# Releasing the first FFN weights earlier, and holding x and conditioning loads back until they have landed, in an eight-core streaming-encoder kernel

## Chip, cores, metric

One Trainium2 chip, all 8 cores, one launch. Each core computes its own 2048 tokens (a quarter of one of two sequences), with 512 tokens of left context as "block 0"; blocks 1 to 4 are its own tokens. The metric is device time of the slowest core, in microseconds (us). Executions in which one die ran visibly slower at a lower granted clock ("slow state"; in one of 1922.9 us the four cores of one die had a mean clock of 0.815 to 0.817 and those of the other 0.971 to 0.980) are left out of every ratio below; where a median includes one, the text says so.

## The reference, cut to what matters

```python
cc = silu(c)
mod = (cc @ w_ada + b_ada)             # 9 x 1024 conditioning values per sequence
sh1, sc1, gt1, ... = mod
h = rms_norm(x, g_ffn1) * (1 + sc1) + sh1
x = x + 0.5 * gt1 * (silu(h @ w_in[:, :2816]) * (h @ w_in[:, 2816:])) @ w_out
# ... token mixing (chunk-band attention and pooling), then a second FFN of the same form
```

Everything here happens in the first 165 us of some 1660: the conditioning values of the first FFN, the first norms, and the first hidden group of the first FFN.

## The kernel before

Names used below. `w_ada` is stored as 72 "rows" of 128 x 1024. One **dot** on DVE turns one row into 128 conditioning values; dots are counted from 0, so dot 2 is the third. Rows 0 to 15 of the early order give shift and scale of the first FFN and must be done before any hidden unit is complete; rows 16 to 23 give its gate, which is first needed when the first group's outputs are added. `w1i` are the input weights of the first FFN: chunk 0 and chunk 1 each hold two hidden tiles (`jj` 0 and 1), each with an a part and a b part. A **unit** is one hidden tile for one block: 16 matmuls. The first group's input units (5 blocks x 4 units) use chunks 0 and 1 only. x0 to x4 are the five blocks of x; x2, x3 and x4 are 2 MB loads. `w1o` are the output weights of the first FFN, `w_pg` is a small weight of the later token mixing. In the profile lines, `arena` is the one SBUF buffer that holds all tiles, `ps` is PSUM, and the line numbers are those of the helpers that record an operation: L179 matmul, L185 and L186 ScalarE activation, L196 a dot, L215 a load.

```python
    for i in range(16):                                   # early conditioning
        dots.append(ada_dot(aorder[i], ADA_R[i % 6]))     # DVE
        if i + 6 < 16:
            ada_load(aorder[i + 6], ADA_R[i % 6], "d_a%d" % (i % 6))   # SP queue
        # [cut: per pair of dots, scale and shift; statistics and norm of x0, x1]
    for i in range(2):
        ada_load(16 + i, ada_slot(16 + i), "d_b%d" % i)
    for b in range(2, 5):
        P.load("sp", XB[b - 1][:, :, :], xT[b], "d_x%d" % b)
# [cut]
        def wi_load(split=None):                          # POOL queue, casts to bf16
            # [cut]
            if split is not None:
                for jj in range(nt):
                    for s, o in ((sa, 0), (sb, NJ)):
                        P.load("pool", ..., deps=[split[jj]])
                return
            for s, o in ((sa, 0), (sb, NJ)):
                P.load("pool", piece(s)[:, 0:nt, :], ...)
        def pre():
            wi_load(startup)              # chunk 0: waits for dots 2 and 11
        def body():
            wi_load()                     # chunk 1
            wo_load(0)                    # w1o of the first group, needed at about 150 us
            for bi, b in enumerate(blocks):
                for k in range(2):
                    for jj in range(2):
                        unit(k, jj, b, spread if bi == k == jj == 0 else None)
                        side["g0"](bi, 2 * k + jj)        # norms of x2..x4, later dots
# [cut]
    def g0_1(bi, u):
        g0_norms(4 * bi + u, N1)          # x2: squares after unit 1, statistics matmuls after unit 2
        if bi >= 1 and u % 2 == 0:
            ada_step()                    # one later dot, and the load of the row after next
# [cut]
    pre1()
    P.load("pool", WPG[:, :, :], ..., "d_wpg", deps=[dots[15]])
    body1()
```

The kernel's helper gives each engine its instructions in program order. `g0_norms`: behind unit 1 (units count from 0) ACT squares x2, and behind unit 2 PE has the statistics matmuls that read these squares. So PE reaches unit 3 only after x2 is there.

## Time and profile before

| | before |
|---|---|
| median time | 1668.4 us (fast runs 1667.7 to 1671.0) |
| PE busy, share of the chain of waits | 92% of the span, 83% |
| PE waiting for w1i, per core | 14.0 to 16.0 us |
| start of unit 1 / unit 3 / end of the first group's input units | 64.7 / 88.1 / 162.8 us |
| from there to the last matmul | 1491.2 us |

The last two rows are counted matmul by matmul: TensorE runs the same 7085 matmuls in the same order, so the start of the 58th, 94th and 386th can be compared between runs. Two of the eight traces have 140 matmul records missing; such means are over the six full traces.

PE's waits in the first 160 us of the slowest core (core 4):

```profile
PE ps L179 <- ACT arena L186: 25.2, 7, 14.6
PE ps L179 <- ACT arena L185: 23.7, 13, 11.9
PE ps L179 <- DMA arena<-w1i: 16.0, 3, 6.8
```

The three waits for w1i in the timeline of that core's PE (start, length, instructions, and in brackets the idle time before and what ended it):

```profile
59.94 0.59 PE L179 MATMUL ps<-arena 128*128 128x512 bf16 x2 [1.85 <-ACT arena L186]
65.26 3.41 PE L179 MATMUL ps<-arena 128*128 128x512 bf16 x8 [4.73 <-DMA arena<-w1i]
73.16 3.57 PE L179 MATMUL ps<-arena 128*128 128x512 bf16 x8 [4.49 <-DMA arena<-w1i]
83.49 16.82 PE L179 MATMUL ps<-arena 128*128 128x512 bf16 x65 [6.76 <-DMA arena<-w1i]
```

Unit 0 ends at about 60.5 us; unit 1 gets its a half at 65.26, its b half at 73.16, and chunk 1 lands only at 83.49. Eight matmuls take 3.41 or 3.57 us here, twice their usual time (they start every 427 ns; at full clock, later on the same core, every 216 ns). The table by stretches shows why (columns: stretch, its length, busy us and count for PE, PEld, DVE, ACT, POOL, then granted clock, DMA busy share, GB/s):

```profile
50.00:60.00 10.00, 3.92 (x18) 1.34 (x17) 7.35 (x16) 5.46 (x8) 2.33 (x4) 1.00 1.02 292
60.00:70.00 10.00, 3.94 (x10) 1.09 (x10) 0.69 (x1) 5.73 (x8) 2.30 (x4) 0.66 1.03 301
70.00:80.00 10.00, 3.57 (x8) 1.02 (x8) 0.69 (x1) 1.25 (x2) 0.00 (x0) 0.59 1.00 254
80.00:90.00 10.00, 6.51 (x18) 2.39 (x19) 0.09 (x1) 0.60 (x1) 0.00 (x0) 0.56 0.96 161
90.00:100.00 10.00, 10.00 (x48) 4.57 (x47) 1.59 (x3) 7.08 (x8) 0.00 (x0) 1.00 0.01 3
```

The granted clock, the first of the last three numbers, falls to about 0.6 from 60 to 90 us (0.66, 0.59, 0.56) and returns to 1.00. Its records hold only 1.00 and 0.50, and each spell of half clock in the first 165 us lasts 3.4 us or a multiple of it. In this trace gaps of 4.5 to 6.8 us were followed by matmuls of double length, and the gap of 1.9 us was not (two matmuls in 0.59 us).

The DMA engines are full from 50 to 85 us (a busy share of 0.98 to 1.08 in each 5 us), and most of what fills them is x2 to x4: 6.3 of the 9.9 MB written from 47 to 85 us. They are issued at 47.1 to 49.2 us and land after 16, 23 and 28 us; w1i issued at 51.7 lands after 13.5 and 20.8 us, and at 59.5 after 23.9 and 25.9 us.

### The profile page before, as it was taken

Reading aid. Unit: us, or ns where it says so; the run is one execution under the profiler, and the core shown is the slowest. Engines: PE = TensorE matmul, PEld = TensorE weight load, DVE = VectorE, ACT = ScalarE, POOL = GpSimd, SP = SyncE. Lnnn points to the kernel's source line nnn. Section 1 sums busy time; section 2 is a strip of 40 time slices with the busy share of each in tenths; the row PEclk is TensorE's granted clock in tenths of the full one; section 3 lists DMA queues with packets and bytes.
Section 4 is the critical chain, followed back from the end, with each engine's and each line's share of the span. In section 5 each row is a group of like instructions: output and inputs, shape, how many; then the busy total and the mean of one; then the engine's idle time right before and its main releaser. Section 6 shows DMA issues by size and latency. Waiting matters only on the chain.

```text
span 1667.4 us, 20421 instructions; the slowest of 8 cores (1653.6 to 1667.4 us)
## 1 busy us (share of the span) xinstructions
PE 1537.1 (92%) x7085; PEld 672.7 (40%) x7085; DVE 820.2 (49%) x1300; ACT 480.2 (29%) x615; POOL 95.7 (6%) x191
## 2 busy tenths in 40 slices
PE   1498999999999998898799998799999999999999
PEld 0133444444444443342244432244434444444444
DVE  4446736447346346735745445645456161613416
ACT  3354010110110114655644165644150101011110
POOL 0101000010010000000011100001101000001000
PEclk9799999999999998898899998799999999999999
DMA  9923353161370353030054530044504313104005
GB/s 280 267 54 88 62 123 80 39 140 33 90 145 10 89 127 75 1 51 1 1 89 76 88 51 1 1 89 77 88 1 76 51 26 57 26 14 83 13 1 202
DMA packets 45938, 119.50 MB, mean 72 GB/s; under 512 B 4112, under 2 KB 4240, under 8 KB 45328
## 3 DMA queue, kind: packets, MB, share of 16 engines
q0 software_dynamic: 31152, 59.91, 21.8%
q1 hardware_dynamic: 14688, 58.30, 10.7%
q8 instruction: 60, 0.98, 0.2%
q14 instruction: 38, 0.31, 0.1%
HBM read 169.70 MB, written 8.39 MB: 107 GB/s over the span
## 4 chain that ended last, share of the span: by engine, by line
PE 83%; DVE 5%; ACT 4%; DMA 4%; issue 3%; SPq 0%; DVEq 0%; ACTq 0%; POOL 0%
PE ps L179 83%; ACT arena L185 3%; DMA arena<-w_ada 2%; DVE arena L189 2%; DVE arena L194 2%; DMA arena<-w1i 1%; DVE arena L196 1%; ACT arena L186 1%; SPq L215 0%; DVE arena L209 0%; ACT L185 0%; ACT L186 0%; DVE arena L201 0%; DVEq L173 0%; DVE arena L205 0%
## 5 line engine op out<-in xcount | busy, mean ns | idle before, releaser
L179 PE MATMUL ps<-arena 128*128 128x512 bf16 (+5 forms) x7085 | 1537.1, 380 | 126.4 <-ACT arena L185 37.1
L179 PEld LDWEIGHTS ps<-arena 128*128 128x128 bf16 (+1 forms) x7085 | 672.7, 99 | 990.3 <-issue 246.6
L185 ACT ACTIVATE arena<-ps 128x512 bf16<-128x512 f32 (+4 forms) x368 | 271.0, 745 | 911.1 <-PE ps L179 903.7
L189 DVE TENSOR_TENSOR arena<-arena,ps 128x512 bf16<-128x512 bf16 (+1 forms) x230 | 175.2, 762 | 560.8 <-PE ps L179 493.3
L194 DVE SCALAR_TENSOR_TENSOR arena<-ps,arena 128x512 f32<-128x512 f32 (+1 forms) x410 | 315.5, 774 | 155.3 <-PE ps L179 80.2
L185 ACT ACTIVATE arena<-arena 128x1024 bf16<-128x1024 f32 (+2 forms) x105 | 95.2, 929 | 37.5 <-PE ps L179 15.8
L196 DVE SCALAR_TENSOR_TENSOR arena<-arena 128x1024 f32<-128x1024 f32 x72 | 87.8, 1220 | 32.4 <-DMA arena<-w_ada 18.3
L189 DVE TENSOR_TENSOR arena<-arena 128x512 bf16<-128x512 bf16 (+9 forms) x191 | 89.9, 494 | 27.0 <-ACT arena L185 19.6
L186 ACT ACTIVATE arena<-arena 128x512 bf16<-128x512 f32 (+1 forms) x84 | 57.5, 715 | 124.8 <-DVE arena L194 103.1
L194 DVE SCALAR_TENSOR_TENSOR arena<-arena 128x512 f32<-128x512 f32 (+2 forms) x114 | 78.9, 728 | 1.9 <-ACT arena L186 0.5
L215 POOL DMA_DIRECT2D arena<-w1i x26 | 17.1, 660 | 520.0 <-PE ps L179 470.2
L189 DVE TENSOR_TENSOR arena<-ps,arena 64x512 bf16<-64x512 f32 x32 | 22.0, 688 | 43.4 <-ACT arena L185 43.0
L215 POOL DMA_DIRECT2D arena<-w3i x24 | 16.3, 678 | 380.3 <-PE ps L179 380.3
L215 POOL DMA_DIRECT2D arena<-w_in x28 | 19.8, 707 | 297.3 <-PE ps L179 297.3
L186 ACT ACTIVATE arena<-ps,arena 128x1024 f32<-128x1024 f32 (+1 forms) x32 | 29.6, 926 | 17.4 <-PE ps L179 17.2
L185 ACT ACT_TABLE_LOAD x14 | 18.0, 1283 | 43.7 <-PE ps L179 36.5
L201 DVE TENSOR_SCALAR arena<-arena 128x512 bf16<-128x512 f32 (+2 forms) x45 | 19.8, 441 | 6.0 <-DMA arena<-cst 1.0
L212 POOL MEMSET arena<- 64x128 bf16 x64 | 11.9, 198 | 166.8 <-ACT arena L185 166.8
L186 ACT ACT_TABLE_LOAD x12 | 15.4, 1283 | 13.4 <-PE ps L179 13.3
L201 DVE TENSOR_SCALAR arena<-ps,arena 128x512 bf16<-128x512 f32 (+2 forms) x25 | 15.6, 638 | 4.6 <-PE ps L179 4.4
L209 DVE CAST arena<-ps 128x256 bf16<-128x256 f32 x32 | 12.0, 418 | 4.3 <-PE ps L179 4.0
L215 POOL DMA_DIRECT2D arena<-w_o x8 | 5.6, 704 | 73.8 <-PE ps L179 73.8
(14 smaller groups left out, 51.5 us busy)
## 6 DMA issues: line engine op xcount, KB each, us to landing
arena<-w_ada SPq DMA_DIRECT2D x72, 512.0 KB, 4.3
arena<-w_in POOLq DMA_DIRECT2D x28, 512.0 KB, 6.1
arena<-w3i POOLq DMA_DIRECT2D x20, 512.0 KB, 6.3
arena<-w1i POOLq DMA_DIRECT2D x18, 512.0 KB, 10.0
outT<-arena SPq DMA_DIRECT2D x16, 512.0 KB, 3.0
arena<-xT SPq DMA_DIRECT2D x3, 2048.0 KB, 23.0
arena<-w1o POOLq DMA_DIRECT2D x10, 512.0 KB, 16.5
arena<-w3o POOLq DMA_DIRECT2D x10, 512.0 KB, 9.6
```

What stands on the lines that cost most here:

```text
L179: return self.op("pe", lambda e: e.matmul(out, lhsT=lhsT, rhs=rhs, start=start, stop=stop), reads=[lhsT, rhs], writes=[out])
L185: return self.op("act", lambda e: e.activation(out=out, in_=in_, func=func, scale=scale), r, [out])
L186: return self.op("act", lambda e: e.activation(out=out, in_=in_, func=func, bias=bias, scale=scale), r, [out])
L189: return self.op(eng, lambda e: e.tensor_tensor(out=out, in0=in0, in1=in1, op=op), [in0, in1], [out])
L194: return self.op("dve", lambda e: e.scalar_tensor_tensor(out=out, in0=in0, scalar=scalar, in1=in1, op0=op0, op1=op1), r, [out])
L196: return self.op("dve", lambda e: e.scalar_tensor_tensor(out=out, in0=in0, scalar=scalar, in1=in1, op0=op0, op1=op1, accum_out=accum), r, ...
L201: return self.op(eng, lambda e: e.tensor_scalar(out=out, in0=in0, scalar1=s1, scalar2=None, op0=op0), r, [out])
L209: return self.op(eng, lambda e: e.tensor_copy(out=out, in_=in_), [in_], [out])
L212: return self.op(eng, lambda e: e.memset(out, v), [], [out])
L215: return self.op(q, lambda e: e.dma_start(out=out, in_=in_), [], [out], deps, sem)
```

## The change

Its intent: the weights that PE is about to need should not share the DMA engines with x blocks and rows needed later. The weights are released earlier (dots 1, 7, 11, 13), chunk 1 goes ahead of `w_pg`, and x2, rows 16 and 17, x3 and x4 are issued only when chunk 1 has landed. As rows 16 and 17 come later, the eight dots that fell into the last four blocks (two each) become nine in the last three (three each).

```diff
@@ (behind the early conditioning loop)
-    for i in range(2):
-        ada_load(16 + i, ada_slot(16 + i), "d_b%d" % i)
-    for b in range(2, 5):
-        P.load("sp", XB[b - 1][:, :, :], xT[b], "d_x%d" % b)
@@ def wi_load
-                for jj in range(nt):
-                    for s, o in ((sa, 0), (sb, NJ)):
-                        P.load("pool", ..., deps=[split[jj]])
-                return
+                return [P.load("pool", ..., deps=[split[2 * k + jj]])
+                        for jj in range(nt) for s, o in ((sa, 0), (sb, NJ))]
@@ def body
-            wi_load()
+            if startup is None:
+                wi_load()
@@ def g0_1
-        if bi >= 1 and u % 2 == 0:
+        if bi >= 2 and u < 3:
             ada_step()
@@
-                      startup=[dots[2], dots[11]], ...
+                      startup=[dots[1], dots[7], dots[11], dots[13]], ...
     pre1()
+    last = pre1()
+    P.load("sp", XB[1][:, :, :], xT[2], "d_x2", deps=last)
+    for i in range(2):
+        ada_load(16 + i, ada_slot(16 + i), "d_b%d" % i)
+    for b in range(3, 5):
+        P.load("sp", XB[b - 1][:, :, :], xT[b], "d_x%d" % b)
```

More of the change, by code (lines that the diff above doesn't have):

```diff
@@ L558, in wi_load @@
             if split is not None:
-                for jj in range(nt):
-                    for s, o in ((sa, 0), (sb, NJ)):
-                        P.load("pool", piece(s)[:, jj:jj + 1, :],
+                return [P.load("pool", piece(s)[:, jj:jj + 1, :],
                                w_i[o + j0 + jj:o + j0 + jj + 1].rearrange("j p c -> p j c"),
-                               "d_w%d" % s if jj == 0 else "d_wy%d" % s, deps=[split[jj]])
-                return
+                               "d_w%d" % s if jj == 0 else "d_wy%d" % s, deps=[split[2 * k + jj]])
+                        for jj in range(nt) for s, o in ((sa, 0), (sb, NJ))]
             for s, o in ((sa, 0), (sb, NJ)):
@@ L612, in pre @@
         def pre():
-            wi_load(startup)
+            return wi_load(startup)
         def body():
-            wi_load()
+            if startup is None:
+                wi_load()
             wo_load(0)
@@ L713, in build_nc @@
     pre1, body1 = ffn(w1i, w1o, 0, [0, 1, 2, 3, 4], True, dict(g0=g0_1, g0end=g0end_1, unit=unit_1, op=lambda: None),
-                      [(0, 1), (2, 3)], (4, 5), startup=[dots[2], dots[11]], tail=tail_1,
+                      [(0, 1), (2, 3)], (4, 5), startup=[dots[1], dots[7], dots[11], dots[13]], tail=tail_1,
                       spread=lambda kt: warm(5) if 2 <= kt <= 6 else None)
     pre1()
+    last = pre1()
[4 more added lines that the diff above has]
+        P.load("sp", XB[b - 1][:, :, :], xT[b], "d_x%d" % b)
     P.load("pool", WPG[:, :, :], w_pg.rearrange("(g c) d -> c g d", c=128), "d_wpg", deps=[dots[15]])
```

## The prediction

About 17 us, less 1 to 2, is some 15 us, from 1668.4 to 1653 us. The 1 to 2 us for "clock phases" were the estimate; the trace shows what one such phase cost (eight matmuls in 3.41 to 3.57 us instead of about 1.7, so 1.7 to 1.9 us), not that a gap of 2 to 4 us brings one.

> **What bounds the kernel now.** TensorE: the profile has PE busy 92% of a 1667.4 us span, and the chain of waits is 83% PE. The exception is the start. In the waits of the slowest core's first 160 us, PE lost 48.9 us to ACT and 16.0 to three w1i landings (timeline: 4.73 us before 65.26, 4.49 before 73.16, 6.76 before 83.49; 14.0 to 16.0 on all cores). PE then also runs slowly: granted clock 0.66, 0.59, 0.56 in 60-90 us, 1.00 around it; eight matmuls take 3.41 to 3.57 us instead of about 1.7. [...]
>
> The weights are late because of what shares the engines: DMA busy share is 1.0 from 10 to 85 us, and three 2 MB x loads (issued 47.1 to 49.2, landing after 16, 23, 28 us) overlap them: w1i issued at 51.7 lands after 13.5 and 20.8 us, at 59.5 after 23.9 and 25.9 us, against 8.5 and 11.5 us for the first pair.
>
> **What the change does.** No byte, PE or ACT instruction is added. x2, then conditioning rows 16 and 17, x3, x4 are issued only when chunk 1 of w1i has landed. The w1i pieces are released at dots 1, 7, 11, 13 instead of 2, 11, then after 15; chunk 1 comes as four loads ahead of w_pg. The conditioning dots of the second block move to later blocks (three per block).
>
> **Costs, estimates from the trace.**
> - Releasing the first pair at 19.5 instead of 28.9 us puts 1 MB of reads among x1 and w_ada 2 to 5. Dot 2 waited 17.35 us for w_ada and starts at 27.0; I expect +2 us (1 to 3), shifting the DVE-bound dot chain: unit 0 ends near 62.5 instead of 60.5.
> - The second pair, released near 42 us, lands near 51; w_ada has 4 to 6 us of slack there, so no further delay.
> - Chunk 1, released near 53 and 56.6 us with q1 almost empty, has landed near 61.
> - x2 is issued at 61 and lands near 70 (7.3 us for its bytes plus latency).
> - PE: units 0, 1, 2 end at 62.5, 66, 69.5, without a w1i wait and at full clock. Then PE stands at the statistics matmuls of block 2, which need x2 and two squares of 1.0 us: a new gap of 2 to 4 us. Unit 3 starts near 73; before, near 90.3.
> - x3 and x4 are due near 84 and 97 us and land near 80 and 87; rows 16 and 17 are first used near 90.
> - Moving dots: about 0.
>
> All of it is on the critical path and should reach the end: about 17 us, less 1 to 2 for clock phases after the new gap.
>
> **Prediction: 1653 us, 8 in 10 between 1648 and 1660. Faster by over 2%: 0.01; within 2%: 0.98; slower: 0.01.**
>
> **What would show each step.** Waits of PE for w1i in the first 160 us: 16.0 to under 2 us. Granted clock in 60-70: near 1.0. Dot 2 at 28 to 30 us. x2 issued at 59 to 63, landing in under 10 us. A new PE gap before ACT's squares at 68 to 73 us. The first group's input units (end about 152 us) over 14 to 18 us earlier, the rest unchanged in length.
>
> **What would make it wrong.** The first pair delaying the dots by over 3 us; x2 landing after 73[...]; x3 late, a second gap near 87 us; three dots per block stalling PE.

## The result, and the profile after

| | before | after |
|---|---|---|
| median time, us | 1668.4 | 1662.4 (of four runs, one of them slow; the three fast ones 1660.0 to 1663.8) |
| ratio of the fast runs, 95% interval | | 0.9957 (0.9937 to 0.9976) |
| PE waiting for w1i, every core | 14.0 to 16.0 | none recorded |
| start of unit 1, us | 64.7 | 62.5 |
| start of unit 3, us | 88.1 | 78.6 |
| end of the first group's input units, us | 162.8 | 155.8 |
| from there to the last matmul, us | 1491.2 | 1492.0 |

Ratios here are the mean time of one kernel's fast runs over that of the other's in the same rounds, so they are not quite the ratio of the medians beside them. The change is faster by 0.4%, which is about 7 us, where 15 us had been forecast.

PE's waits after (core 5, the slowest of the profiled run): the line for w1i is gone, and both waits for ACT have grown.

```profile
PE ps L179 <- ACT arena L185: 29.4, 13, 10.9
PE ps L179 <- ACT arena L186: 28.1, 8, 17.5
```

What took its place, from the timeline of that core. SPq issues x2, POOL issues w1o, ACT squares x2 once it has landed, PE then starts the statistics matmuls and unit 3:

```profile
63.02 7.50 PE L179 MATMUL ps<-arena 128*128 128x512 bf16 x34 [1.86 <-ACT arena L186]
64.84 0.71 POOL L215 DMA_DIRECT2D arena<-w1o  x1 [2.27 <-ACT arena L186]
64.86 0.33 SPq L215 DMA_DIRECT2D arena<-xT  x1
...
75.96 2.01 ACT L185 ACTIVATE arena<-arena 128x1024 bf16<-128x1024 f32 x2 [7.86 <-DMA arena<-xT]
...
77.16 13.19 PE L179 MATMUL ps<-arena 128*128 128x512 bf16 x50 [6.64 <-ACT arena L185]
```

From 63.02 us PE runs the end of unit 0 and units 1 and 2 to about 70.5 us without a break and then stands still for 6.64 us. ACT's bracket names the cause: 7.86 us until x2 landed. x2 was issued at 64.86 us, when chunk 1 had landed, and was in use 11 us later. The table by stretches shows the full clock at 60 to 70 us, and part of the loss again at 70 to 90:

```profile
50.00:60.00 10.00, 5.74 (x25) 2.18 (x24) 8.77 (x18) 4.11 (x7) 2.11 (x4) 1.00 0.69 175
60.00:70.00 10.00, 8.14 (x39) 3.55 (x38) 2.95 (x6) 6.78 (x10) 2.16 (x3) 1.00 0.80 152
70.00:80.00 10.00, 3.36 (x10) 0.90 (x9) 0.69 (x1) 4.04 (x5) 0.00 (x0) 0.74 1.02 262
80.00:90.00 10.00, 10.00 (x44) 4.36 (x43) 1.16 (x2) 5.42 (x7) 0.00 (x0) 0.92 1.01 292
90.00:100.00 10.00, 9.20 (x43) 3.91 (x42) 7.03 (x12) 5.93 (x9) 0.00 (x0) 1.00 0.59 205
```

On the eight cores x2 was issued at 62.4 to 65.3 us and landed 10.0 to 14.5 us later; on the full traces PE's new gap is 5.3 to 11.0 us.

A second, smaller loss is early. The third dot's lines of DVE, first before, then after (with the next dot's line):

```profile
27.04 1.23 DVE L196 SCALAR_TENSOR_TENSOR arena<-arena 128x1024 f32<-128x1024 f32 x1 [6.91 <-DMA arena<-w_ada]
```
```profile
28.08 1.23 DVE L196 SCALAR_TENSOR_TENSOR arena<-arena 128x1024 f32<-128x1024 f32 x1 [8.08 <-DMA arena<-w_ada]
...
31.46 1.22 DVE L196 SCALAR_TENSOR_TENSOR arena<-arena 128x1024 f32<-128x1024 f32 x1 [2.15 <-DMA arena<-w_ada]
```

These are cores 4 and 5, but the mean of the eight cores says the same: the third dot starts 1.0 us later (27.3 instead of 26.2), and the next, which ran straight behind it before, now waits for its own row (2.15 us in the last line). Over the six full traces the first hidden matmul (the 17th of all) moved from 41.2 to 44.3 us.

### The profile page after: what moved, and what is told of

Read it like the earlier page. It is cut to its first block, busy times and chain, and to the rows that moved or that the text cites. A ratio compares the mean times of both kernels' runs of the same rounds, so it can differ in the third digit from the quotient of the medians.

```text
span 1658.2 us, 20429 instructions; the slowest of 8 cores (1647.0 to 1658.2 us)
## 1 busy us (share of the span) xinstructions
PE 1533.5 (92%) x7085; PEld 671.5 (40%) x7085; DVE 819.9 (49%) x1300; ACT 480.7 (29%) x615; POOL 96.2 (6%) x193
## 4 chain that ended last, share of the span: by engine, by line
PE 83%; DVE 5%; ACT 5%; DMA 3%; issue 3%; SPq 0%; DVEq 0%; ACTq 0%; POOL 0%; POOLq 0%
PE ps L179 83%; ACT arena L185 3%; DVE arena L189 2%; DVE arena L194 2%; DMA arena<-w_ada 1%; ACT arena L186 1%; DMA arena<-w_ap 1%; DVE arena L196 1%; DMA arena<-xT 1%; SPq L215 0%; DVE arena L209 0%; DMA arena<-w1i 0%; ACT L185 0%; ACT L186 0%; DVE arena L201 0%
## 5 line engine op out<-in xcount | busy, mean ns | idle before, releaser
L189 DVE TENSOR_TENSOR arena<-arena 128x512 bf16<-128x512 bf16 (+9 forms) x191 | 89.9, 494 | 27.9 <-ACT arena L185 20.7
L196 DVE SCALAR_TENSOR_TENSOR arena<-arena 128x1024 f32<-128x1024 f32 x72 | 87.8, 1220 | 31.3 <-DMA arena<-w_ada 30.6
L215 POOL DMA_DIRECT2D arena<-w3i x24 | 16.2, 676 | 380.3 <-PE ps L179 380.3
L186 ACT ACT_TABLE_LOAD x12 | 15.4, 1283 | 13.4 <-PE ps L179 13.3
L201 DVE TENSOR_SCALAR arena<-ps,arena 128x512 bf16<-128x512 f32 (+2 forms) x25 | 15.6, 638 | 4.7 <-PE ps L179 4.4
## 6 DMA issues: line engine op xcount, KB each, us to landing
arena<-xT SPq DMA_DIRECT2D x3, 2048.0 KB, 24.6
arena<-w3o POOLq DMA_DIRECT2D x10, 512.0 KB, 10.2
```

The costliest lines, as they stand in the source:

```text
L186: return self.op("act", lambda e: e.activation(out=out, in_=in_, func=func, bias=bias, scale=scale), r, [out])
L189: return self.op(eng, lambda e: e.tensor_tensor(out=out, in0=in0, in1=in1, op=op), [in0, in1], [out])
L196: return self.op("dve", lambda e: e.scalar_tensor_tensor(out=out, in0=in0, scalar=scalar, in1=in1, op0=op0, op1=op1, accum_out=accum), r, ...
L201: return self.op(eng, lambda e: e.tensor_scalar(out=out, in0=in0, scalar1=s1, scalar2=None, op0=op0), r, [out])
L215: return self.op(q, lambda e: e.dma_start(out=out, in_=in_), [], [out], deps, sem)
```

## The experiments

The theory when they began: most of the missing gain is PE's new wait for x2; the early release of the first pair of weights costs 3 us; the regrouped dots cost about 2 us. Rivals: that the small costs are the whole story; that the hold, or the earlier release alone, carries the gain. In the expectations "105th matmul" is the twelfth of unit 3's sixteen, so it stands behind unit 3's start by 2.4 us in the kernel before and by 2.9 to 4.3 in the change (full traces), where part of it runs at half clock. In their text "mean of the cores" took all eight traces; the table below takes the full ones. All outputs are right.

| run | ratio to before (95%) | unit 1 starts | unit 3 starts | unit 3 to end of input units |
|---|---|---|---|---|
| before | 1 | 64.7 | 88.1 | 74.7 |
| the change, first result | 0.9957 (0.9937-0.9976) | 62.5 | 78.6 | 77.2 |
| the change, again | 0.9943 (0.9927-0.9958) | 63.5 | 82.9 | 77.6 |
| x2 not held | 0.9882 (0.9865-0.9899) | 63.6 | 71.4 | 78.5 |
| x2 in four pieces | 0.9941 (0.9924-0.9958) | 63.9 | 80.5 | 78.6 |
| first pair at dot 2 | 0.9920 (0.9901-0.9939) | 60.3 | 78.6 | 77.2 |
| release only, no hold | 0.9944 (0.9926-0.9961) | 63.5 | 84.2 | 77.8 |
| hold only, old release | 0.9968 (0.9953-0.9983) | 60.5 | 87.8 | 77.4 |
| w1o behind x2 | 0.9913 (0.9895-0.9931) | 63.3 | 78.0 | 77.2 |
| old dots | 0.9961 (0.9942-0.9979) | 63.9 | 81.4 | 76.3 |
| w1o behind x2, pair at dot 2 | 0.9898 (0.9879-0.9917) | 60.6 | 75.5 | 77.3 |
| x2 not held, pair at dot 2 | 0.9870 (0.9848-0.9892) | 60.9 | 68.6 | 80.5 |
| ordered, four dots in last block | 0.9887 (0.9867-0.9908) | 60.5 | 68.5 | 74.1 |
| ordered, three dots per block | 0.9843 (0.9830-0.9857) | 60.6 | 68.6 | 76.9 (75.8 without the two cores at low clock, see below) |

Times are us from the span's start, from one profiled fast run each. The first two rows come from the chip of the first result; on the later chips the kernel before ran 1672.8 to 1674.7 us instead of 1668.4 and has no profile there. So profiles of the variants are best compared with each other, and with the kernel before by the ratios. The difference matters: "hold only" ends its input units 2.4 us later than the profile of the kernel before, and still beats it in the same rounds. Why the later chips run the kernel before slower is not shown. From the end of the input units to the last matmul every run but the last two took 1490 to 1493 us, so what happens in the first 165 us is all that these variants change.

### x2 not held

```diff
+    P.load("sp", XB[1][:, :, :], xT[2], "d_x2")       # behind the early rows, as before
     ada_j = [16]
...
     last = pre1()
-    P.load("sp", XB[1][:, :, :], xT[2], "d_x2", deps=last)
     for i in range(2):
-        ada_load(16 + i, ...)
+        P.load("sp", ada_slot(16 + i), w_ada[16 + i], "d_b%d" % i, deps=last)
```

> The change, but x2 alone is issued where the kernel before had it (about 49 us, right behind the last early conditioning row); rows 16 and 17, x3 and x4 still wait for the first group's weights. Theory (most of the missing gain is a new wait of PE for x2, because x2 is issued at 62 to 65 us and lands 10 to 14.5 us later): the PE idle of 5 to 12 us behind unit 2 (ACT's squares waiting for x2 until 72.5 to 79.9 us) falls under 1 us, unit 3 (105th matmul) starts 7 to 9 us earlier than in the change (mean of the cores), w1i still costs PE under 2 us, and the time is about 1654 us, 8 us under the change. Rival (the early first pair of weights, which started the dots 3 us late, and the three dots per block, which cost 2 us later, are what is missing): unit 3 moves by less than 3 us and the time stays at 1660 to 1663.

Measured: ratio 0.9882, 1653.2 us. Unit 3 starts at 71.4 us, and w1i still costs PE nothing. PE's timeline of the slowest core:

```profile
62.46 23.04 PE L179 MATMUL ps<-arena 128*128 128x512 bf16 x106 [1.85 <-ACT arena L186]
89.00 1.53 PE L179 MATMUL ps<-arena 128*128 128x512 bf16 x3 [3.50 <-ACT arena L185]
```

From 62.46 us 106 recorded matmuls run in one piece; the gap for x2 is gone. x2, issued near 49 us, landed 13.1 to 15.6 us later, before it was needed, and chunk 1, which now shared the engines with it, landed 8.4 to 11.9 us after its issue instead of 3.8 to 6.7. That was early enough. The theory holds and the rival (under 3 us) is out. A new small wait shows in the second line: ACT waits up to 3.0 us for x3, which the hold delays, and PE stands 3.50 us before 89 us.

### x2 in four pieces

```diff
-    P.load("sp", XB[1][:, :, :], xT[2], "d_x2", deps=last)
+    for p in range(4):
+        P.load("sp", XB[1][:, 2 * p:2 * p + 2, :], xT[2][:, 2 * p:2 * p + 2, :], "d_x2%d" % p, deps=last)
```

> The change, but x2 is loaded in four pieces of 512 KB, each with its own semaphore, so that ACT's first square needs a quarter of the bytes. Same hold. Theory (PE waits for the bytes of x2): the first square starts 5 to 7 us earlier than in the change (at 67 to 72 instead of 72.5 to 79.9 us), PE's gap behind unit 2 shrinks to 2 to 5 us, time 1657 to 1659. Rival (fixed latency of the landing, or something other than x2 releases PE): the first square and the time move by less than 1.5 us.

Measured: 0.9941, no better than the change. ACT's squares of core 5 (each now waits for its own piece):

```profile
75.78 1.06 ACT L185 ACTIVATE arena<-arena 128x1024 bf16<-128x1024 f32 x1 [7.70 <-DMA arena<-xT]
78.33 1.06 ACT L185 ACTIVATE arena<-arena 128x1024 bf16<-128x1024 f32 x1 [1.49 <-DMA arena<-xT]
...
83.02 2.18 ACT L185 ACTIVATE arena<-arena 128x1024 bf16<-128x1024 f32 x2 [3.15 <-DMA arena<-xT]
```

On core 0 the first square came at 68.42 us as hoped, but its last at 80.02; on core 5 the first came no earlier than before and the last at 83 to 84. This expectation failed. The packet records suggest why. x2 as one load moves in packets of 16 KB, in pieces of 4 KB rows in packets of 4 KB, and w1o beside it in packets of 2 KB (as written in bf16; 4 KB as read). In the kernel before core 4 started 29 x packets and 44 weight packets from 60 to 62 us, and 200 and 202 from 60 to 72; in the first profile of the change, from 70 to 76 us, core 0 started 85 and 87; and in the repeated change, from 72 to 80 us, core 1 started 27 to 33 x packets and 26 to 38 weight packets in each 2 us: about one for one. So in these three profiles a whole x load took about 8 written bytes for each weight byte. With packets of 4 KB the ratio was 2: in the first profile of the change, core 5, 153 packets of rows 16 and 17 went beside 153 weight packets from 76 to 80 us, and from 74 to 76 us of this run (core 5) x2 got 178 GB/s beside 88 GB/s of w1o. What makes the counts near-equal is not shown. My reading of these counts is that smaller packets gave away x2's share.

### First pair of weights at dot 2

```diff
-   startup=[dots[1], dots[7], dots[11], dots[13]]
+   startup=[dots[2], dots[7], dots[11], dots[13]]
```

> The change, but the first pair of w1i waits for dot 2 as in the kernel before, not for dot 1. Theory (1 MB of weights released at 19.5 us delays conditioning row 2 by about 1 MB of transfer and with it the dot chain): dot 2 starts within 1 us of the kernel before (27 us), everything up to the x2 wait is 2 to 4 us earlier, time 1658 to 1660. If instead the chain's start is unaffected by that pair, dot 2 stays where the change has it and the time at 1662.

Measured: 0.9920. The third dot ends 0.5 us later than before (27.9 against 27.4; the change 28.3 and 29.3), the 17th matmul starts at 41.9 instead of 44.3 or 45.2, and unit 1 at 60.3: the early pair does cost about 3 us. Unit 3 however starts at 78.6 us, as in the first profile of the change. At that point I took this to mean that a slower x2 had eaten the 3 us (it landed after 10.2 to 16.2 us); the second profile of the change, with unit 3 at 82.9, shows that x2's landing scatters by more than that, so this run alone does not show it.

### Release only, no hold

```diff
     # x2..x4 and rows 16, 17 issued behind the early rows, as in the kernel before
+    for i in range(2): ada_load(16 + i, ...)
+    for b in range(2, 5): P.load("sp", XB[b - 1][:, :, :], xT[b], "d_x%d" % b)
...
-    last = pre1()
-    # [the held loads]
+    pre1()
```

> Only the new release of the weights (dots 1, 7, 11, 13, four loads of chunk 1) and the moved conditioning dots; x2 to x4 and rows 16 and 17 are issued as in the kernel before, without the hold. Theory (x in 16 KB packets pushes out the weights' packets): chunk 0 lands in time, but chunk 1, released at 54 to 58 us among x2 to x4, lands at 70 to 78 us; PE waits 5 to 12 us for w1i and nothing for x2; time 1660 to 1666, near the change. Rival (the earlier release alone removes the wait for weights): PE waits under 2 us for w1i, time about 1652.

Measured: 0.9944, as good as the whole change. PE's waits (core 5): the loss for w1i is back, at 9.7 us where the kernel before had 15.6 on this core.

```profile
PE ps L179 <- ACT arena L186: 27.4, 8, 17.4
PE ps L179 <- ACT arena L185: 23.3, 12, 11.5
PE ps L179 <- DMA arena<-w1i: 9.7, 3, 4.3
```

Chunk 1's first pair lands 13.3 to 21.9 us after its issue, its second pair 24.6 to 27.2, that is at 83 to 86 us and not by 78 as expected. Unit 3 starts at 84.2 us. The packet records of the kernel before show what such loads meet: on core 4, from 62 to 66 us, x had 1.16 of the 1.28 MB written. The theory holds and the rival is out: the earlier release alone does not remove the wait for weights.

### The change again, and w1o behind x2

The change was repeated on the chip of the next runs.

> The change itself, unchanged, on the same chip as the next three, so that they can be compared with it. Ratio to before 0.9957 as in the first result (0.994 to 0.9976); start of the 105th matmul (the twelfth of unit 3) at 82.3 us in the mean of the cores, within 1 us.

```diff
-            wo_load(0)
+            wo_load(0, deps)       # deps = [x2's load]
```

> The change, but the first two w1o loads (2 MB of reads, issued at 63 to 66 us, not needed before about 150 us) wait for x2's landing. In the change and in the run with the first pair at dot 2, x2 took 10 to 11 us to land where it was issued with or before w1o and 12 to 16 us where w1o came up to 1.6 us before it. Theory (x2's landing shares the engines with w1o, so a start of the chain that is 3 us earlier was eaten by a slower x2): x2 lands in 7.5 to 9.5 us on every core, the 105th matmul starts 2 to 5 us earlier than in the change, time 3 to 4 us less. Rival (x2 is slow for another reason, such as the neighbouring core's traffic or the rows and x3 behind it in its own queue): x2 keeps 10 to 14.5 us and the time stays.

Measured: the change again 0.9943, w1o behind x2 0.9913. The expectation of the 105th matmul within 1 us failed: it came at 86.9 instead of 82.3 us (eight traces). The reason is in the same profile. On cores 4 and 5 x2 was issued with w1o or up to 0.3 us before it and landed after 11.2 and 10.7 us; on the other six w1o had been issued 0.9 to 1.3 us earlier, and x2 landed after 14.8 to 16.7 us. Core 1, first the repeated change, then with w1o behind x2:

```profile
65.06 0.70 POOL L215 DMA_DIRECT2D arena<-w1o  x1 [2.28 <-ACT arena L186]
...
66.19 0.33 SPq L215 DMA_DIRECT2D arena<-xT  x1
...
82.65 2.00 ACT L185 ACTIVATE arena<-arena 128x1024 bf16<-128x1024 f32 x2 [14.33 <-DMA arena<-xT]
```
```profile
64.92 0.33 SPq L215 DMA_DIRECT2D arena<-xT  x1
...
73.76 2.00 ACT L185 ACTIVATE arena<-arena 128x1024 bf16<-128x1024 f32 x2 [5.98 <-DMA arena<-xT]
74.21 1.40 POOL L215 DMA_DIRECT2D arena<-w1o  x2 [11.97 <-DMA arena<-xT]
```

In the first, w1o leads by 1.1 us and ACT waits 14.33 us for x2; the packet records have no x2 packet before 72 us, although x2 was issued at 66.19, and w1o moved at 87 to 103 GB/s from 68 to 72 us. On all six such cores the first x2 packet came 3.6 to 5.9 us after the issue, on cores 4 and 5 after 1.0 and 1.9 us. The first profile of the change agrees: on core 1, with w1o 0.9 us ahead, the first x2 packet came after 4.4 us and x2 landed after 14.5; on the other seven cores, with w1o at most 0.5 us ahead, after 0.9 to 2.0 and 10.0 to 12.2 us. In the second x2 lands in 8.8 us. With w1o out of the way x2 landed in 7.8 to 11.2 us on all cores (7.5 to 9.5 had been expected), unit 3 started 4.9 us earlier than in the repeated change and the mean ratio fell by 0.0030 (the intervals just touch). So w1o is one part of x2's slow landing, and its order against x2 is a race between a dot chain and a weight landing. It is not the whole gap: even with w1o out of the way PE stood 3.8 to 7.6 us for x2.

### Old dots

```diff
-        if bi >= 2 and u < 3:
+        if bi >= 1 and u % 2 == 0:
```

> The change, but the conditioning dots of the first group are spread as before (two in each of blocks 2 to 5 of the five, none moved). From unit 3 to the end of the first group's input units the kernel before took 75.1 us, the change 77.5 and the run without the hold 78.1. Theory (three dots in a row on DVE cost about 2 us): that stretch returns to 75 to 76 us unless rows 16 and 17 come too late for the second block's first dot (then a DVE wait for w_ada of some us near 85 us shows and it stays at 77 or more). Time 0 to 2 us below the change. Rival (the stretch is longer for the hold's sake, by x3 or x4 landing late): no change.

Measured: unit 3 to the end of the input units 76.3 us instead of 77.6, and no DVE wait for a row. The regrouping costs about 1.3 us of the 2.5 to 2.9 by which that stretch grew. The clock records show how: PE's idle time in the stretch is about the same in all three (before 8.9 us, the change again 7.9, old dots 8.8), but the time at half clock is 1.7, 9.5 and 5.4 us, and half of it is lost (a matmul started every 427 ns there, every 216 ns at full clock). Why the three dots bring more such spells is not shown. The whole time does not show the gain: the fast runs averaged 1666.4 us against 1663.4 of the repeated change, where 0 to 2 us less had been expected (0.9961; the intervals overlap, and x2's race scatters by more). On the time this run is inconclusive.

### Hold only, old release of the weights

```diff
+   startup=[dots[2], dots[11]], chunk 1 as two loads behind w_pg; x2.. held for chunk 1
```

> Only the hold (x2 first, then rows 16 and 17, x3, x4 wait for chunk 1) and the moved dots; the weights are released as before (dots 2 and 11; chunk 1 as two loads behind w_pg). Theory: the second pair, released near 51 us, lands near 56 to 57; chunk 1, released at 59.5, lands at 66 to 67; x2 is issued there and lands at 76 to 78, so unit 3 stands within 2 us of where the change has it (78.8 us): the earlier release of the weights gains next to nothing because x2 decides. Time within 3 us of the change. Rival (the early release carries the gain): unit 3 is over 4 us later than in the change and the time above 1664.

Measured: 0.9968, 1668.1 us. Chunk 1 takes 7.7 to 11.9 us to land, longer than expected, with w1o issued beside it; x2 is issued at 70.5 to 72.5 us and needs another 12.6 to 14.0. Unit 3 starts at 87.8 us, 4.9 us later than in the repeated change on the same chip, and the time is 4 us more. The theory (within 2 us) failed here, and the rival is right on both counts: how early chunk 1 comes matters, because x2 is chained to it. The hold alone keeps a small gain (the interval excludes 1), the release alone has as much as the whole change (0.9944 against 0.9943 and 0.9957), and the two together are no better than the release: the hold, with x2 in it, turns the wait for w1i into a wait for x2.

### Both small repairs with x2 still held

The first pair at dot 2 and w1o behind x2.

> The change with both: first pair of w1i at dot 2, and the first two w1o loads waiting for x2. Theory (the dot chain started 3 us late because of the early pair, and in the run that undid only this, x2 gave the 3 us back because w1o got ahead of it): now both effects add, dot 2 ends near 27.8, x2 lands in 8 to 11 us and the 105th matmul starts near 79 us, 3 us before the run with w1o behind x2 alone (82.0); ratio to before about 0.989. Rival (x2's landing is pinned by something else, so an earlier issue only lengthens it): 105th matmul at 81 to 82.5 us again, ratio 0.991 to 0.992.

Measured: 0.9898; the 105th matmul at 79.3 us against 82.0 with w1o behind x2 alone (eight traces), unit 3 at 75.5 against 78.0. The effects add, in the ratio too. With w1o out of the way, an earlier issue of x2 was an earlier landing here.

### x2 not held, first pair at dot 2

> x2 without the hold, and the first pair of w1i at dot 2. Theory: nothing waits for x2, so the 3 us of the dot chain now reach PE: unit 1 starts near 60.5 instead of 63.7 us, the 105th matmul near 71 instead of 73.9, ratio to before 0.986 to 0.987. Rival (chunk 1, which then has x2 beside it, becomes the wait): PE waits over 2 us for w1i and the 105th matmul stays above 73.

Measured: 0.9870; unit 1 at 60.9 and unit 3 at 68.6 us, 2.8 us before the run with x2 free alone; no wait for w1i. But the stretch behind it grew to 80.5 us: ACT now waits 0.9 to 4.8 us for x3 (up to 3.0 with the pair at dot 1), and the hold releases x3 behind rows 16 and 17 while w1o runs beside them.

### The ordered version

```diff
+    P.load("sp", XB[1][:, :, :], xT[2], "d_x2")                   # not held
     last = pre1()                                                 # pair 0 at dot 2
+    x3 = P.load("sp", XB[2][:, :, :], xT[3], "d_x3", deps=last)   # x3 ahead of the rows
     # rows 16, 17, then x4
-    body1()
+    body1([x3])                                                   # first w1o loads behind x3
-        if bi >= 2 and u < 3:
+        if bi == 4 or (bi >= 2 and u % 2 == 0):
```

> The version meant to be best: x2 without the hold, first pair at dot 2, x3 ahead of rows 16 and 17 in the held queue, the first two w1o loads behind x3's landing, conditioning dots in blocks 3 to 5 as two, two and four. Expected beside the previous run: the waits of ACT for x3 (1 to 3 us near 87 us in the run with x2 free) go, and unit 3 to the end of the first group's input units (78.8 us there, 75.1 before) falls to 75 to 77; ratio to before about 0.984 to 0.986. If the order of the held loads does not matter, it equals the previous run.

Measured: the stretch fell to 74.1 us as expected, but the ratio is only 0.9887: what followed took 1498 us. Core 0, at the end of the first group's inputs:

```profile
148.26 1.23 DVE L196 SCALAR_TENSOR_TENSOR arena<-arena 128x1024 f32<-128x1024 f32 x1 [5.12 <-DMA arena<-w_ada]
...
151.05 9.19 PE L179 MATMUL ps<-arena 128*128 128x512 bf16 x34 [3.60 <-DVE arena L194]
```

The last of the eight gate dots waits 5.12 us for its row, which was issued only two units earlier among the next weights; PE waits 3.60 us for the first output that needs the gate. I took that for my dot schedule and not the load order; the next run tests it. PE's remaining later waits in that run (9.9 us for DVE on core 0 from 140 to 740 us, 4.7 before) I did not pursue.

Last, the same load order with the change's own dots:

> The ordered version (x2 free, first pair at dot 2, x3 ahead of rows 16 and 17, w1o behind x3) with the change's own dots (three in each of blocks 3 to 5). The run before this one put four dots in the last block; its last row then landed 5.1 us late on DVE behind the next weights and PE waited 3.6 us for it. Theory (only the dots spoilt it): that wait is gone, the first group's input units end near 143 to 145 us, the rest lasts 1498 to 1501 us as in all other runs, ratio to before 0.983 to 0.985. Rival (the ordered loads themselves push the later stages back): the rest stays above 1503 us and the ratio at 0.987 or more.

Measured: 0.9843 (0.9830 to 0.9857), 1648.3 us. It beats both kernels: 26 us under the kernel before in the same rounds. The first group's input units end at 145.5 us, and no w1i wait and no gap for x2 or x3 is left; core 1 shows one piece of 106 matmuls from 60.16 us:

```profile
60.16 23.42 PE L179 MATMUL ps<-arena 128*128 128x512 bf16 x106 [0.38 <-ACT arena L186]
```

This run and the one before it moved x3 and w1o together, so which of the two removed the wait for x3 is not separated. What follows took 1484 to 1496 us on four of the six full traces and 1503 and 1511 on cores 6 and 7. Those two had a lower clock in this one execution, which took 1666.6 us where the other five fast ones took 1646.6 to 1648.7 (with it, the ratio of the means of all fast runs would be 0.9861); the stretch from 140 to 240 us, core 7, then core 1:

```profile
140.00:240.00 100.00, 100.00 (x395) 42.00 (x393) 49.22 (x72) 8.37 (x14) 6.34 (x9) 0.84 0.42 78
```
```profile
140.00:240.00 100.00, 100.00 (x465) 45.34 (x464) 53.75 (x79) 11.35 (x19) 4.21 (x6) 1.00 0.53 104
```

0.84 against 1.00, with PE busy throughout in both. The clock records have both cores at 0.81 for 159 us, from 66 to 225 us, and no other core; over the whole run their mean clock is 0.960 and 0.958, that of the others 0.975 to 0.981. So the long rest in this profile is the clock of two cores and not the load order. Without these two the input units end at 143.8 us, within the expected 143 to 145.

## Why the prediction was wrong

The forecast was 1653 us, 1648 to 1660; measured were 1662.4. The direction and the chain of causes were right, but one step of the chain was sized far too small, and a second term somewhat.

- **Right: the waits for w1i go.** Predicted under 2 us, measured none on any core, and full clock at 60 to 70 us (1.00).
- **Right, at the edge of its range: the first pair delays the dots.** Predicted 2 us (1 to 3) and unit 1 near 62.5; the 17th matmul came 3.1 us later and unit 1 at 62.5. Undoing it gave 3 us back in three runs.
- **Wrong, and the step that failed: "x2 is issued at 61 and lands near 70 (7.3 us for its bytes plus latency)", "a new gap of 2 to 4 us. Unit 3 starts near 73".** x2 was issued at 62.4 to 65.3 us, since the last pair of chunk 1 was issued 0.9 us later than I had it in the mean (55.9 to 58.6 against 56.6 us) and took 4.4 to 6.7 us; it landed 10.0 to 14.5 us after that, the gap was 5.3 to 11.0 us, and unit 3 started at 78.6 us in the mean (and at 82.9 in a second profile). In the means x2 was issued at 64.1 instead of 61 us and took 11.5 instead of 9 us to land: 3.1 us of the error are the late issue and 2.5 us the slow landing. From the landing to unit 3 it took 3.0 us, as predicted. The 7.3 us is 2 MB at the rate of x in the kernel before, in a queue already running (on core 4 x3 and x4 landed 7.7 and 6.7 us after the x load before them). The prediction leaves out w1o, which was issued within 0.9 us of x2 on every core; in the repeated change it came first on six cores, and there x2 took 14.8 to 16.7 us. The run with x2 unheld shows the size of the whole term: 7.2 us against the first profile of the change (78.6 to 71.4), 11.5 against the second, and 10 to 13 us of the time (0.9882 against 0.9943 to 0.9957).
- **Wrong by size: "less 1 to 2 for clock phases", "moving dots: about 0".** The gap brought the low clock back (0.74 and 0.92 at 70 to 90 us), and unit 3 to the end of the input units grew by 2.5 us. By the clock records that is all clock: time at half clock in that stretch rose from 1.7 to 7.3 us in the mean, which at half rate (427 against 216 ns from matmul to matmul) costs 2.8 us, while PE's idle time there fell by 0.4 us. About two fifths of the rise follow x2's gap; the rest are later spells of 3.4 us near 118 and 143 us, fewer with the old dots.
- **Right: the rest is unchanged.** 1492.0 against 1491.2 us. Nothing was lost later.

The sum, on full traces: 9.5 us gained at unit 3, less 2.5 behind it, is the 7.0 us at the end of the input units and, within the scatter of the slowest core, the 7 us of the time. My 17 us were reckoned from the slowest core, where unit 3 stood at 90.4 instead of 88.1 us; that is another 2 us of the difference.

My list of what would make it wrong named this case ("x2 landing after 73"), but the range gave it too little room: the benefit hung on one load that the change itself puts at the end of a serial chain (dots, chunk 1, x2, squares, statistics).

## What to carry to other kernels

When a load is made to wait for another's landing, ask who needs the held load first, and leave that one out of the hold: here holding x2 gave back what the hold won, and holding only what comes after x2 more than doubled the gain. A load's duration read from a queue that was already running (7.3 us for 2 MB, the prediction's estimate) was too short for the same load issued anew: 7.8 to 11.2 us with w1o out of the way, 10.0 to 16.7 us beside w1o in the two profiles of the change. And order by first use can be worth much without moving fewer bytes: the last version moves the same bytes as the first and takes 26 us less.

## What the runs measured of the hardware, and what stays open

- Packets: x in rows of 16 KB moved about 8 bytes for each written byte of w1o in rows of 2 KB, as the rows went in near-equal numbers (85 and 87 on core 0 of the change, from 70 to 76 us); splitting x2 into loads with rows of 4 KB cut that to 2 (178 beside 88 GB/s) and gained nothing (0.9941).
- A short lead: in the repeated change a 2 MB load issued 0.9 to 1.3 us behind loads of another queue landed after 14.8 to 16.7 us and moved its first packet 3.6 to 5.9 us after its issue; issued with or ahead of them it landed after 10.7 to 11.2 us, first packet after 1.0 to 1.9. The runs show the effect, not its mechanism.
- The clock of the cores: in the profiles of both kernels (fast runs) granted clock is 1.00 for 1512 to 1533 us of every span, and 0.5 in all other records. In the last run a third value showed (0.81, 159 us long), on cores 6 and 7 only, while cores 4 and 5 of their die did not have it. In the slow executions, left out above, whole dies were low: in one of 1922.9 us (the change) the four cores of one die had a mean granted clock of 0.815 to 0.817 and those of the other 0.971 to 0.980; in one of 1878.9 us (the kernel before) all eight had 0.834 to 0.866. No trace of a slow execution was kept, so what lowers the clock there, and on the two cores of the last run, stays open.
- Half clock: spells in the first 165 us of the two kernels began with PE busy for 0 to 1.4 us of the 3.4 us before them (1.37 us on core 7 of the kernel before, at 123.9 us). Gaps of the same length differed: one of 2.8 us near the end of the input units was followed by a spell on all eight cores in the change but on three of eight in the kernel before. What decides this is not shown.
